# Down projection blocks of seven products: product 3 inside the chain, and six more low parts per group made by ScalarE and an accumulating transfer

## The chip, the cores and the metric

The kernel runs on one core of a Trainium2 chip, in one launch. The metric is the device time of an execution in microseconds. A core has a matrix engine (PE), a vector engine (DVE), a scalar engine (ACT), GpSimd (POOL) and a synchronising engine (SP). They run at the same time, each one through its own list of instructions in order, and wait for each other by semaphores. SP issues the loads of weights, POOL the transfers that add to what is in their destination. PE writes to PSUM, in banks that other engines read.

## The reference

Two layers, each an attention-like mixing part and a gated feed-forward part, on 512 tokens of width 1024, all in float32. The change is in the feed-forward part, which both layers have:

```python
f = rmsnorm(h, ln_ffn_pre[layer])
f = (jax.nn.silu(f @ w_ffn_gate[layer]) * (f @ w_ffn_up[layer])) @ w_ffn_down[layer]
h = h + rmsnorm(f, ln_ffn_post[layer])
```

The hidden width D_FF is 2816, 22 blocks of 128.

## The kernel before

**Parts.** PE is fed with pairs of tiles: a float32 tile is split into a high part that PE's input format holds (whi, fhi) and a low part, the rest (wlo, flo). A product of two such pairs is three matmuls: high by high, high by low, low by high (`mm3`, lines 191 to 193). The usual split (`split`, line 239) is a cast on ACT and a subtraction on DVE. A second form (`split_aside`, lines 1151 to 1153) leaves DVE out: ACT casts, ACT writes the negated high part into the low tile, and POOL issues a transfer that adds the source to it. Before, only the last two of the four splits of the first pair in a group are made that way. Pairs of weights lie in eight buffers that are used in turn, so they can be made eight ahead of PE.

**Blocks of seven.** Gate, up and down products are 2 by 2 blocks, multiplied with seven block products instead of eight (after Winograd). Two hidden blocks with all eight blocks of width are one `Seven` for gate and one for up: their raw weights come by SP into tiles raw, DVE forms sums and differences of the four quadrants (lines 1041 to 1046), and PE makes product 1, 7, 2, 6, 4, 3, 5 in this order; product 7, into tile e, needs the parts of the difference s3.

**Groups.** Hidden blocks 2 to 21 are taken in five groups of four. A group is two pairs of Sevens; in the first four groups a down block of seven (`down_sevens`) follows, which adds the group's share of the result into eight tiles y, of 128 tokens by 512 columns (ys[token block][half]; ys[0][0], ys[0][1], ys[1][0], ... are y_2471 to y_2478 in the first layer). Two layers make eight such down blocks. The block has two units: a for the first pair of hidden blocks, whose raw weights come in tiles raw, and b for the second, with four tiles wd. `Inner.combine` makes the activations' sums and parts, `DownSeven` the weights'. A product of a unit is six matmuls 512 wide, onto two PSUM banks: chain (yc), shared (ys), lows (yl) and, before, ups (yu).

**Getting sums out.** `put` copies a bank to a tile yo on ACT and lets POOL issue one accumulating transfer of 256 KB for each tile y that the sum belongs to (line 1229). `final` adds a bank to its y tile on DVE (line 1232); where a put into that y tile is under way, DVE waits for it to land.

**The order** on each engine is fixed when the kernel is built, by a scheduler that goes by data and buffers and by the order in which the code is written; PE and DVE may get rows of different products interleaved. Transfers of POOL are issued in the order of its list.

Of the kernel before, what the change touches and what calls it, by code (L numbers as in the profile page):

```python
# [40 lines left out]
def hybrid(ctx: ExitStack, tc: tile.TileContext, i: dict, out: bass.AP):  # L41
# [20 lines left out]
    def plain(s, shape=(P, T), dt=F32):  # L62
        return yp.tile(list(shape), dt, tag="y", name=name(s))
# [174 lines left out]
    def split(src, hi, lo, eng=None):  # L238
        last_parts[:] = A.copy(hi, src), (eng or V).tensor_sub(lo, src, hi)  # L239
# [873 lines left out]
    def feed_forward(layer, phase, xp, meanwhile=None):  # L1113
# [34 lines left out]
        def split_aside(src, hi, lo, aside):  # L1148
            if not aside:
                return split(src, hi, lo)  # L1150
            A.copy(hi, src)
            A.activation(lo, hi, AF.Copy, scale=-1.0)
            G.dma_start(lo, src, accum_op=ALU.add)

        class Inner:

            def __init__(self, k, aside):
                self.k, self.aside, self.u = k, aside, {}

            def __call__(self, row, u):  # L1160
                self.u[row] = u
# [3 lines left out]
            def combine(self, u0, u1):  # L1165

                left, right = (slice(*c) for c in HALVES)
                first = tp.tile([P, 2, 256], F32R, tag="acc", name=name("b11"), bufs=2)
                split(u0[:, left], first[:, 0, :], first[:, 1, :])
                second, both, other = [(act("fhi"), act("flo")) for _ in range(3)]  # L1170
                split(u1, *second)
                V.tensor_sub(u0[:, left], u0[:, right], u0[:, left])
                V.tensor_sub(u0[:, right], u1[:, right], u0[:, right])
                V.tensor_sub(u1[:, right], u0[:, left], u1[:, right])
                V.tensor_add(u1[:, left], u1[:, right], u1[:, left])
                split_aside(u0, *both, self.aside)
                split_aside(u1, *other, self.aside)
                half = lambda pair, c: tuple(t[:, c] for t in pair)
                self.x = {1: (first[:, 0, :], first[:, 1, :]), 2: half(second, left), 3: half(second, right),
                          4: half(other, left), 5: half(both, left), 6: half(other, right), 7: half(both, right)}  # L1180

        class DownSeven:

            def __init__(self, pair, spare):
                self.x = pair.x
                if spare:
                    a11, a12, a21, a22 = (plain("wd").rearrange("p (m c) -> p m c", m=4) for _ in range(4))
                    for n, a in enumerate((a11, a12, a21, a22)):
                        last_load[0] = nc.sync.dma_start(
                            a, i["w_down"][layer, 4 * (n // 2) : 4 * (n // 2) + 4, :, pair.k + n % 2, :].rearrange("m p c -> p m c"))  # L1190
                else:
                    raws = []
                    for dh in range(2):
                        raw = wp.tile([P, 1024], F32, tag="raw", name=name("raw"), bufs=4)
                        last_load[0] = nc.sync.dma_start(
                            raw.rearrange("p (m c) -> p m c", m=4),
                            i["w_down"][layer, 4 * dh : 4 * dh + 4, :, pair.k : pair.k + 2, :].rearrange("m p k c -> p m (k c)"))
                        raws.append(raw.rearrange("p (m k c) -> p m k c", m=4, k=2))
                    a11, a12, a21, a22 = (r[:, :, x, :] for r in raws for x in range(2))
                self.w = {4: a22}  # L1200
# [4 lines left out]
                self.w[2] = self.parts(a12)  # L1205
                V.tensor_sub(a11, a11, a21)
                V.tensor_add(a12, a11, a12)
                self.w.update({3: a12, 5: a21, 6: a11, 7: s3})

            def parts(self, src):  # L1210
                pair = pair_of_parts()
                split(src, *(t.rearrange("p (m c) -> p m c", m=4) for t in pair))
                return pair

            def product(self, outs, n, start, stop):
                w = self.w[n]
                if n > 2:
                    w = self.parts(w)
                for x, o in enumerate(outs):
                    c = slice(x * P, (x + 1) * P)  # L1220
                    mm3(o, tuple(t[:, c] for t in self.x[n]), w, start, stop, True)

        def down_sevens(pairs):

            def put(x, *where):
                some = prob("yo")
                A.copy(some, x)  # L1227
                for tb, dh in where:
                    G.dma_start(ys[tb][dh], some, accum_op=ALU.add)  # L1229

            def final(x, tb, dh):
                V.tensor_add(ys[tb][dh], x, ys[tb][dh])

            a, b = DownSeven(pairs[0], False), None
            chain = [ps("tr", s="yc") for _ in range(2)]
            a.product(chain, 1, True, False)
            lows = [ps("mm", s="yl") for _ in range(2)]
# [24 lines left out]
            b.product(chain, 5, False, True)  # L1262
            for x in range(2):
                put(chain[x], (x + 2, 0), (x + 2, 1))
            b.product(shared, 4, False, True)
            for x in range(2):
                final(shared[x], x, 1)

        fs = [(act("fhi"), act("flo")) for _ in range(2)]

# [19 lines left out]
                A.copy(ys[tb][dh], o)  # L1290

        for gi, (k0, k1) in enumerate(groups):
            fs, pairs = [], []
            for m in range(k0, k1, 2):
                if meanwhile and m == k1 - 2 and gi == len(groups) - 1:
                    next(meanwhile)
                if gi < len(groups) - 1:
                    pairs.append(Inner(m, m < k1 - 2))
# [19 lines left out]
            down_sevens(pairs)  # L1318


    def layer_b(phase, fp):
# [297 lines left out]
```

## Time and profile before

| what | value |
|---|---|
| median of 3 runs | 1107.26 us (1107.19 to 1495.4) |
| profiled execution, its own time | 1105.52 us |
| its span, first to last instruction | 1103.8 us |
| mean granted clock of PE in it | 0.995 |
| PE busy | 1082.3 us (98%) |
| DVE busy | 972.7 us (88%) |
| ACT busy | 752.5 us (68%) |
| POOL busy | 107.5 us (10%) |
| accumulating puts y<-yo | 80, of 256 KB, 7.4 us from issue to landing (median) |
| low parts flo by transfer | 16, of 256 KB, 3.3 us (median) |

A row of a group of instructions reads: line, engine, operation, output<-inputs, how often; durations in ns (smallest, median, largest) or busy us and mean ns; then the idle time before and what ended it. A row of the timeline reads: start and duration in us, engine, line, operation, tiles, count, and in brackets the idle time before it and what ended it. A row of waits reads: engine and line, what it waited for, us in total, number of waits, the longest.

### The profile page before, as it was taken

How to read it: one execution, taken by the hardware profiler on the slowest of the kernel's cores; microseconds unless marked ns; L12 is line 12 of the kernel's file. 1: busy time of each engine (PE TensorE's matmuls, PEld its weight loads, DVE VectorE, ACT ScalarE, POOL GpSimd, SP SyncE). 2: the span in 40 equal slices, each digit the busy share in tenths (PEclk: the TensorE clock that was granted, in tenths of full speed). 3: DMA queues.
4: the chain of work that ended last, by engine and by line, in shares of the span. 5: the costliest groups of instructions: out<-in, count | busy, mean ns of one | idle time of the engine just before them, and what ended most of it. 6: DMA issues, size and time to landing. Idle time of an engine off the chain costs nothing.

```text
span 1103.8 us, 19831 instructions
## 1 busy us (share of the span) xinstructions
PE 1082.3 (98%) x7266; PEld 986.1 (89%) x7267; DVE 972.7 (88%) x1942; ACT 752.5 (68%) x1588; POOL 107.5 (10%) x136
## 2 busy tenths in 40 slices
PE   9999999999999999899999999999999999999998
PEld 8998889998979898898988998889997989899996
DVE  7879759899989999897967789968999999999986
ACT  7776578666656667577846788868666756666664
POOL 0000000003030212101000000000003020210200
PEclk9999999999999999999999999999999999999999
DMA  7521331338474573836122555541347566383832
GB/s 269 161 79 58 115 115 39 115 96 210 134 159 144 123 206 92 204 133 204 44 91 77 139 133 134 141 127 39 98 113 161 145 148 178 86 220 96 188 118 77
DMA packets 86297, 143.85 MB, mean 130 GB/s; under 512 B 7028, under 2 KB 50056, under 8 KB 86200
## 3 DMA queue, kind: packets, MB, share of 16 engines
q1 hardware_dynamic: 71480, 116.57, 34.1%
q0 software_dynamic: 14016, 25.70, 13.1%
q8 instruction: 57, 0.93, 0.3%
q10 hardware_dynamic: 704, 0.32, 0.1%
q14 instruction: 40, 0.33, 0.1%
HBM read 105.23 MB, written 2.10 MB: 97 GB/s over the span
## 4 chain that ended last, share of the span: by engine, by line
PE 77%; DVE 10%; DMA 6%; ACT 3%; issue 2%; POOL 1%; SPq 0%; DVEq 0%; ACTq 0%
DMA y<-yo 5%; PE y L191 5%; PE y L192 5%; PE y L193 4%; PE a L191 4%; PE a L192 4%; PE a L193 4%; PE ps L191 4%; PE ps L193 4%; PE ps L192 4%; PE e L193 3%; DVE wlo L239 3%; PE e L192 3%; PE e L191 3%; PE x L192 3%; PE x L193 3%
## 5 line engine op out<-in xcount | busy, mean ns | idle before, releaser
L239 ACT CAST whi<-raw 128x512 fp32r<-128x512 f32 x444 | 260.4, 619 | 116.1 <-DVE raw L1045 46.2
L239 DVE TENSOR_TENSOR wlo<-raw,whi 128x512 fp32r<-128x512 f32 x444 | 291.9, 687 | 20.4 <-ACT whi L239 19.8
L192 PE MATMUL x<-xslo,whi 128*128 128x256 f32 x320 | 90.6, 283 | 0.0
L191 PE MATMUL x<-xshi,whi 128*128 128x256 f32 x320 | 90.5, 283 | 0.0
L193 PE MATMUL x<-xshi,wlo 128*128 128x256 f32 x320 | 90.3, 282 | 0.0
L191 PE MATMUL a<-xshi,whi 128*128 128x256 f32 x320 | 89.9, 281 | 0.0
L192 PE MATMUL a<-xslo,whi 128*128 128x256 f32 x320 | 89.8, 281 | 0.0
L193 PE MATMUL a<-xshi,wlo 128*128 128x256 f32 x320 | 89.7, 280 | 0.0
L1229 POOL DMA_DIRECT2D y<-yo x80 | 69.4, 1147 | 195.3 <-ACT yo L1227 173.2
L191 PE MATMUL ps<-xshi,whi 128*128 128x256 f32 (+1 forms) x224 | 68.4, 305 | 0.0
L192 PE MATMUL ps<-xslo,whi 128*128 128x256 f32 (+1 forms) x224 | 66.7, 298 | 0.0
L193 PE MATMUL ps<-xshi,wlo 128*128 128x256 f32 (+1 forms) x224 | 66.3, 297 | 0.0
L193 PEld LDWEIGHTS x<-xshi,wlo 128*128 128x128 f32 x320 | 61.1, 191 | 0.0
L192 PEld LDWEIGHTS x<-xslo,whi 128*128 128x128 f32 x320 | 60.9, 190 | 0.0
L191 PEld LDWEIGHTS x<-xshi,whi 128*128 128x128 f32 x320 | 60.9, 190 | 0.0
L192 PEld LDWEIGHTS a<-xslo,whi 128*128 128x128 f32 x320 | 60.2, 188 | 0.4
L191 PEld LDWEIGHTS a<-xshi,whi 128*128 128x128 f32 x320 | 60.2, 188 | 0.4
L193 PEld LDWEIGHTS a<-xshi,wlo 128*128 128x128 f32 x320 | 60.3, 188 | 0.0
L193 PE MATMUL e<-t3hi,wlo 128*128 128x256 f32 x160 | 46.5, 290 | 12.6 <-DVE wlo L239 12.6
L239 ACT CAST whi<-s 128x512 fp32r<-128x512 f32 x56 | 34.8, 622 | 24.6 <-DVE s L1041 15.4
L191 PE MATMUL y<-whi,mixedhi 128*128 128x512 f32 x128 | 51.3, 400 | 0.0
L192 PE MATMUL y<-wlo,mixedhi 128*128 128x512 f32 x128 | 50.5, 395 | 0.0
(358 smaller groups left out, 3645.0 us busy)
## 6 DMA issues: line engine op xcount, KB each, us to landing
raw<-in_w_gate SPq DMA_DIRECT2D x44, 512.0 KB, 3.9
raw<-in_w_up SPq DMA_DIRECT2D x44, 512.0 KB, 4.2
y<-yo POOLq DMA_DIRECT2D x80, 256.0 KB, 7.4
raw<-in_w_down SPq DMA_DIRECT2D x28, 512.0 KB, 4.6
raw<-in_w_out SPq DMA_DIRECT2D x16, 512.0 KB, 3.8
wd<-in_w_down SPq DMA_DIRECT2D x32, 256.0 KB, 10.5
flo<-s POOLq DMA_DIRECT2D x16, 256.0 KB, 3.3
raw<-in_w_b_q SPq DMA_DIRECT2D x8, 512.0 KB, 4.6
```

What stands on the lines that cost most here:

```text
L191: PE.matmul(o, w[0], x[0], start=start, stop=False, skip_group_check=more)
L192: PE.matmul(o, w[0], x[1], start=False, stop=False, skip_group_check=more)
L193: return PE.matmul(o, w[1], x[0], start=False, stop=stop, skip_group_check=more)
L239: last_parts[:] = A.copy(hi, src), (eng or V).tensor_sub(lo, src, hi)
L1229: G.dma_start(ys[tb][dh], some, accum_op=ALU.add)
```

## The change

Product 3 gets no banks of its own any more. It comes last and is added to the chain, after the chain's sum (products 1, 6 and 5) has been put out to ys[x+2][1]; the chain with product 3 then goes by a final addition into ys[x+2][0]. So the put of the sum 1, 6, 5 has one destination instead of two, and a group has eight puts instead of ten. Products are ordered anew; before b's first product stand three products of a (1, 7, 2) instead of four (1, 2, 7, 3). The sum that product 3 needs, a11 + a12, is formed in `product` once product 2's parts are made. The loads of b's four wd tiles are written ahead of the second pair of Sevens instead of inside the down block.

In each group six low parts change from DVE to ACT and POOL: the other two of the first pair's four splits in `Inner`, and the weights' parts of products 3 and 4 of both units. The latter read raw or wd; in raw, rows of 128 numbers lie apart from each other (128x4x128), in wd they lie together. Before DVE may write on u0 and u1 in `Inner`, the transfers that read them must have landed.

```diff
                 first = tp.tile([P, 2, 256], F32R, tag="acc", name=name("b11"), bufs=2)
-                split(u0[:, left], first[:, 0, :], first[:, 1, :])
+                split_aside(u0[:, left], first[:, 0, :], first[:, 1, :], self.aside)
                 second, both, other = [(act("fhi"), act("flo")) for _ in range(3)]
-                split(u1, *second)
+                split_aside(u1, *second, self.aside)
...
-            def parts(self, src):
+            def parts(self, src, aside=False):
                 pair = pair_of_parts()
-                split(src, *(t.rearrange("p (m c) -> p m c", m=4) for t in pair))
+                split_aside(src, *(t.rearrange("p (m c) -> p m c", m=4) for t in pair), aside)
                 return pair
 
             def product(self, outs, n, start, stop):
                 w = self.w[n]
-                if n > 2:
+                if n == 2:
                     w = self.parts(w)
+                    V.tensor_add(self.a[1], self.a[0], self.a[1])
+                    self.w[3] = self.a[1]
+                elif n != 1:
+                    w = self.parts(w, n in (3, 4))
...
+            a, b = us
+            a.sums(pairs[0])
+            chain, shared, lows = ([ps(t, s=n) for _ in range(2)] for t, n in (("tr", "yc"), ("lg", "ys"), ("mm", "yl")))
             a.product(chain, 1, True, False)
+            a.product(shared, 7, True, False)
             a.product(lows, 2, True, False)
-            shared = [ps(t, s="ys") for t in ("mm", "lg")]
-            a.product(shared, 7, True, False)
-            ups = [ps(t, s="yu") for t in ("lg", "lg")]
-            a.product(ups, 3, True, False)
-            b = DownSeven(pairs[1], True)
+            b.sums(pairs[1])
             b.product(chain, 1, False, True)
             for x in range(2):
                 put(chain[x], (x, 0))
             b.product(shared, 7, False, True)
             for x in range(2):
                 put(shared[x], (x, 1), (x + 2, 1))
-            for u in (a, b):
-                u.product(chain, 6, False, u is b)
+            both(chain, 6)
+            with tc.high_priority():
+                for x in range(2):
+                    A.copy(shared[x], chain[x])
+            b.product(lows, 2, False, True)
+            both(chain, 5)
             for x in range(2):
-                A.copy(shared[x], chain[x])
-            b.product(ups, 3, False, True)
+                put(chain[x], (x + 2, 1))
             for x in range(2):
-                final(ups[x], x + 2, 0)
-            a.product(chain, 5, False, False)
-            a.product(shared, 4, False, False)
-            b.product(lows, 2, False, True)
+                V.tensor_add(ys[x][0], lows[x], ys[x][0])
+            both(shared, 4)
             for x in range(2):
-                final(lows[x], x, 0)
-            b.product(chain, 5, False, True)
+                V.tensor_add(ys[x][1], shared[x], ys[x][1])
+            both(chain, 3)
             for x in range(2):
-                put(chain[x], (x + 2, 0), (x + 2, 1))
-            b.product(shared, 4, False, True)
-            for x in range(2):
-                final(shared[x], x, 1)
+                V.tensor_add(ys[x + 2][0], chain[x], ys[x + 2][0])
```

`both` runs a product of a and then of b.

How the lists move is shown in the third group of the first layer. POOL's list there, before, holds the ten puts of the down block:

```order
L1229 DMA y_2471<-yo_4779 128x512
L1229 DMA y_2473<-yo_4782 128x512
L1229 DMA y_2472<-yo_4795 128x512
L1229 DMA y_2476<-yo_4795 128x512
L1229 DMA y_2474<-yo_4799 128x512
L1229 DMA y_2478<-yo_4799 128x512
L1229 DMA y_2475<-yo_4875 128x512
L1229 DMA y_2476<-yo_4875 128x512
L1229 DMA y_2477<-yo_4879 128x512
L1229 DMA y_2478<-yo_4879 128x512
```

And now, with the low parts of product 4 (raw_4711 for a, wd_4413 for b) and of product 3 (raw_4709, wd_4411):

```order
L1234 DMA y_2471<-yo_4768 128x512
L1234 DMA y_2473<-yo_4771 128x512
L1153 DMA wlo_4854<-raw_4711 128x4x128
L1153 DMA wlo_4865<-wd_4413 128x512
L1234 DMA y_2472<-yo_4784 128x512
L1234 DMA y_2476<-yo_4784 128x512
L1234 DMA y_2474<-yo_4788 128x512
L1234 DMA y_2478<-yo_4788 128x512
L1153 DMA wlo_4878<-raw_4709 128x4x128
L1153 DMA wlo_4889<-wd_4411 128x512
L1234 DMA y_2476<-yo_4845 128x512
L1234 DMA y_2478<-yo_4848 128x512
```

The low part of a's product 3 is the ninth transfer of the block. Six of the eight groups have this order. In the first group of each layer the four low parts stand at places 7, 8, 9 and 12, behind the six puts.

PE's list of the changed kernel, at the turn from product 4 of b (ys) to product 3 of a (yc), where the tiles of those transfers are read:

```order
L191 MATMUL ys_4724<-whi_4864,fhi_4697 128x512
L192 MATMUL ys_4724<-wlo_4865,fhi_4697 128x512
L193 MATMUL ys_4724<-whi_4864,flo_4698 128x512
L191 MATMUL yc_4721<-whi_4877,fhi_4391 128x512
L192 MATMUL yc_4721<-wlo_4878,fhi_4391 128x512
L193 MATMUL yc_4721<-whi_4877,flo_4392 128x512
L191 MATMUL yc_4722<-whi_4877,fhi_4391 128x512
L192 MATMUL yc_4722<-wlo_4878,fhi_4391 128x512
L193 MATMUL yc_4722<-whi_4877,flo_4392 128x512
L191 MATMUL yc_4721<-whi_4888,fhi_4693 128x512
L192 MATMUL yc_4721<-wlo_4889,fhi_4693 128x512
```

The first read of wlo_4878 stands 51 rows behind the last matmul of b's product 1 on yc_4721, whose sum is the first put; the first reads of the two low parts of product 4 stand 39 and 45 rows behind it. In the first group of a layer the first read of the last of the four stands 64 rows behind. Before, DVE wrote the tiles that stand at these places.

DVE's list, before, behind the down block: the final additions from ys stand ahead of the low part of s3 (wlo_4931), which the next Seven's tile e waits for:

```order
L1041 TENSOR_TENSOR s_19_4904<-raw_4895,raw_4897 128x512
L239 TENSOR_TENSOR wlo_4907<-raw_4895,whi_4906 128x512
L1043 TENSOR_TENSOR raw_4897<-raw_4897 128x512
L239 TENSOR_TENSOR wlo_4912<-raw_4895,whi_4911 128x512
L1232 TENSOR_TENSOR y_2472<-ys_4728,y_2472 128x512
L1232 TENSOR_TENSOR y_2474<-ys_4729,y_2474 128x512
L1045 TENSOR_TENSOR raw_4895<-raw_4897,raw_4895 128x512
L239 TENSOR_TENSOR wlo_4931<-s_19_4904,whi_4930 128x512
```

And now (the low part of s3 is wlo_4937):

```order
L239 TENSOR_TENSOR wlo_4913<-raw_4901,whi_4912 128x512
L1045 TENSOR_TENSOR raw_4901<-raw_4903,raw_4901 128x512
L239 TENSOR_TENSOR wlo_4918<-raw_4901,whi_4917 128x512
L1046 TENSOR_TENSOR raw_4901<-raw_4901 128x512
L239 TENSOR_TENSOR wlo_4937<-s_19_4910,whi_4936 128x512
L239 TENSOR_TENSOR wlo_4966<-raw_4901,whi_4965 128x512
L1265 TENSOR_TENSOR y_2472<-ys_4723,y_2472 128x512
L1265 TENSOR_TENSOR y_2474<-ys_4724,y_2474 128x512
```

The two additions have moved behind the low part of s3 and the one after it.

More of the change, by code (lines that the diff above doesn't have):

```diff
@@ L1155, in feed_forward, with __init__ @@
         class Inner:
-            def __init__(self, k, aside):
-                self.k, self.aside, self.u = k, aside, {}
+            def __init__(self, aside):
+                self.aside, self.u = aside, {}
             def __call__(self, row, u):
@@ L1182, in feed_forward, with __init__ @@
         class DownSeven:
-            def __init__(self, pair, spare):
-                self.x = pair.x
+            def __init__(self, k, spare):
                 if spare:
-                    a11, a12, a21, a22 = (plain("wd").rearrange("p (m c) -> p m c", m=4) for _ in range(4))
-                    for n, a in enumerate((a11, a12, a21, a22)):
+                    self.a = [plain("wd").rearrange("p (m c) -> p m c", m=4) for _ in range(4)]
+                    for n, a in enumerate(self.a):
                         last_load[0] = nc.sync.dma_start(
-                            a, i["w_down"][layer, 4 * (n // 2) : 4 * (n // 2) + 4, :, pair.k + n % 2, :].rearrange("m p c -> p m c"))
+                            a, i["w_down"][layer, 4 * (n // 2) : 4 * (n // 2) + 4, :, k + n % 2, :].rearrange("m p c -> p m c"))
                 else:
@@ L1196, in __init__, with sums @@
                             raw.rearrange("p (m c) -> p m c", m=4),
-                            i["w_down"][layer, 4 * dh : 4 * dh + 4, :, pair.k : pair.k + 2, :].rearrange("m p k c -> p m (k c)"))
+                            i["w_down"][layer, 4 * dh : 4 * dh + 4, :, k : k + 2, :].rearrange("m p k c -> p m (k c)"))
                         raws.append(raw.rearrange("p (m k c) -> p m k c", m=4, k=2))
-                    a11, a12, a21, a22 = (r[:, :, x, :] for r in raws for x in range(2))
-                self.w = {4: a22}
+                    self.a = [r[:, :, x, :] for r in raws for x in range(2)]
+            def sums(self, pair):
+                self.x = pair.x
+                a11, a12, a21, a22 = self.a
+                self.w = {2: a12, 4: a22}
                 s3 = temp("s3").rearrange("p (m c) -> p m c", m=4)
@@ L1204, in __init__ @@
                 V.tensor_add(a21, a21, a22)
-                self.w[2] = self.parts(a12)
                 V.tensor_sub(a11, a11, a21)
-                V.tensor_add(a12, a11, a12)
-                self.w.update({3: a12, 5: a21, 6: a11, 7: s3})
-            def parts(self, src):
+                self.w.update({5: a21, 6: a11, 7: s3})
+            def parts(self, src, aside=False):
                 pair = pair_of_parts()
-                split(src, *(t.rearrange("p (m c) -> p m c", m=4) for t in pair))
+                split_aside(src, *(t.rearrange("p (m c) -> p m c", m=4) for t in pair), aside)
                 return pair
@@ L1221, in product, with down_sevens @@
                     mm3(o, tuple(t[:, c] for t in self.x[n]), w, start, stop, True)
-        def down_sevens(pairs):
+        def down_sevens(us, pairs):
             def put(x, *where):
@@ L1229, in put, with both @@
                     G.dma_start(ys[tb][dh], some, accum_op=ALU.add)
[L1231 to L1235, printed above, removed]
+            def both(outs, n):
+                a.product(outs, n, False, False)
+                b.product(outs, n, False, True)
+            a, b = us
+            a.sums(pairs[0])
+            chain, shared, lows = ([ps(t, s=n) for _ in range(2)] for t, n in (("tr", "yc"), ("lg", "ys"), ("mm", "yl")))
             a.product(chain, 1, True, False)
-            lows = [ps("mm", s="yl") for _ in range(2)]
+            a.product(shared, 7, True, False)
             a.product(lows, 2, True, False)
-            shared = [ps(t, s="ys") for t in ("mm", "lg")]
-            a.product(shared, 7, True, False)
-            ups = [ps(t, s="yu") for t in ("lg", "lg")]
-            a.product(ups, 3, True, False)
-            b = DownSeven(pairs[1], True)
+            b.sums(pairs[1])
             b.product(chain, 1, False, True)
@@ L1292, in feed_forward @@
         for gi, (k0, k1) in enumerate(groups):
-            fs, pairs = [], []
+            fs, pairs, downs = [], [], []
             for m in range(k0, k1, 2):
@@ L1297, in feed_forward @@
                 if gi < len(groups) - 1:
-                    pairs.append(Inner(m, m < k1 - 2))
+                    pairs.append(Inner(m < k1 - 2))
+                    if m > k0:
+                        downs.append(DownSeven(m, True))
                 else:
@@ L1317, in feed_forward @@
                                layer == 1)
-            down_sevens(pairs)
+            down_sevens([DownSeven(k0, False)] + downs, pairs)
     def layer_b(phase, fp):
```

## The prediction

> **What bounds the kernel now.** First the busy times of the page, to see which engine has no slack.
>
> ```profile
> span 1103.8 us, 19831 instructions
> PE 1082.3 (98%) x7266; PEld 986.1 (89%) x7267; DVE 972.7 (88%) x1942; ACT 752.5 (68%) x1588; POOL 107.5 (10%) x136
> ```
>
> PE is busy for 98% of the span, and the change neither adds nor removes a matmul. What can be won is PE's idle time, 1103.8 - 1082.3 = 21.5 us, and what a slowed clock costs. What can be lost has no such ceiling. So the second view is what PE waited for.
>
> ```profile
> PE e L193 <- DVE wlo L239: 12.6, 7, 3.0
> PE ys L191 <- ACT fhi L239: 1.4, 2, 0.7
> PE yc L192 <- DVE wlo L239: 1.1, 2, 0.5
> ```
>
> The same view, asked for the stretch around each down block, puts six of the seven waits at e there:
>
> ```profile
> PE e L193 <- DVE wlo L239: 0.6, 1, 0.6
> ...
> PE e L193 <- DVE wlo L239: 2.7, 1, 2.7
> ...
> PE e L193 <- DVE wlo L239: 0.9, 1, 0.9
> ...
> PE e L193 <- DVE wlo L239: 3.0, 1, 3.0
> ...
> PE e L193 <- DVE wlo L239: 1.6, 1, 1.6
> ...
> PE e L193 <- DVE wlo L239: 2.5, 1, 2.5
> ```
>
> They sum to 11.3 us. Right behind the block the next group's first Seven runs product 7 (tile e) before its low part exists. The timeline behind the second down block shows why.
>
> ```profile
> 325.68 0.69 DVE L1232 TENSOR_TENSOR y<-ys,y 128x512 f32<-128x512 f32 x1 [3.12 <-DMA y<-yo]
> 326.29 0.68 DVE L1045 TENSOR_TENSOR raw<-raw,raw 128x512 f32<-128x512 f32 x1
> 326.88 0.69 DVE L239 TENSOR_TENSOR wlo<-s,whi 128x512 fp32r<-128x512 f32 x1
> ...
> 327.62 0.58 PE L193 MATMUL e<-t3hi,wlo 128*128 128x256 f32 x1 [2.74 <-DVE wlo L239]
> ```
>
> DVE stood 3.12 us in the final addition to y[1][1], because an accumulating put into the same tile had not landed. The low part of s3 came next but one behind it, and PE stood 2.74 us. So this wait is not a lack of DVE throughput: DVE takes its work in order, and a late transfer held it. After the three long ones the clock fell.
>
> ```profile
> 318.00:334.00 16.00, 13.26 (x81) 12.23 (x80) 11.62 (x20) 6.55 (x13) 3.46 (x4) 0.89 1.11 256
> 445.00:461.00 16.00, 13.04 (x87) 12.36 (x86) 11.14 (x19) 6.99 (x14) 3.46 (x4) 0.89 1.03 258
> 905.00:921.00 16.00, 13.51 (x87) 12.66 (x86) 11.62 (x21) 6.48 (x14) 3.42 (x4) 0.89 1.08 264
> ```
>
> PEclk, third from the end, is 0.89 in each: (1 - 0.89) x 16 = 1.76 us of clock lost per drop, 5.3 us in all.
>
> Now the resource that the change leans on, the queue of accumulating transfers behind POOL: its issues in the second block, their landings, the same for two later groups of puts (the put of 315.57 and that of 324.82 are the latest of their rows), and a low part made this way in a quiet place.
>
> ```profile
> 310.36 1.75 POOL L1229 DMA_DIRECT2D y<-yo  x2 [16.17 <-ACT yo L1227]
> 313.93 3.51 POOL L1229 DMA_DIRECT2D y<-yo  x4 [1.83 <-ACT yo L1227]
> 321.36 0.85 POOL L1229 DMA_DIRECT2D y<-yo  x1 [3.91 <-ACT yo L1227]
> 324.27 1.74 POOL L1229 DMA_DIRECT2D y<-yo  x2 [2.07 <-DMA y<-yo]
> ...
> L1229 POOL DMA_DIRECT2D y<-yo x3: 1197/1530/1877, 314.5 to 315.6; - x3
> DMA to landing us min/median/max: 9.5/10.6/11.6
> ...
> L1229 POOL DMA_DIRECT2D y<-yo x2: 865/1031/1197, 324.3 to 324.8; - x2
> DMA to landing us min/median/max: 6.9/7.3/7.7
> ...
> L1153 POOL DMA_DIRECT2D flo<-s x1: 853/853/853, 354.8 to 354.8; - x1
> DMA to landing us min/median/max: 3.3/3.3/3.3
> ```
>
> Alone, 256 KB land 3.3 us after issue. In the block the sixth put lands 11.6 us after its own issue, 315.57 + 11.6 - 310.36 = 16.8 us after the first one's, and the ninth 324.82 + 7.7 - 310.36 = 22.2 us after it. The landings come in the order of issue, about 2 us apart. So the transfers stand in one line, and what is issued last waits for all before it.
>
> ```profile
> q0 software_dynamic: 14016, 25.70, 13.1%
> ...
> q0 software_dynamic: 1131, 2.08, 56.2%
> q1 hardware_dynamic: 2318, 2.06, 34.5%
> ```
>
> The columns are packets, MB and share of 16 engines. The first row is the page's: 25.70 MB are 98 pieces of 256 KB, and 0.131 x 1103.8 / 98 = 1.48 us is what one takes of all 16 engines. The other two are for 309 to 330 us: the accumulating queue filled 56.2%, weight loads 34.5%. That is why 1.48 us becomes 2.
>
> **The change part by part.** Edits with one answer first. Two puts fewer per group (16 in all) and product 3 carried on in the chain instead of in two banks of its own: no PE work, the same six copies to yo and six final additions. Six low parts per group leave DVE:
>
> ```profile
> L239 DVE TENSOR_TENSOR wlo<-raw,whi 128x512 fp32r<-128x512 f32 x444 | 291.9, 687 | 20.4 <-ACT whi L239 19.8
> ...
> L239 DVE TENSOR_TENSOR flo<-f,fhi x8: 417/424/427, 186.7 to 781.2; 128x256 fp32r<-128x256 f32 x8
> L1152 ACT ACTIVATE flo<-fhi x16: 626/632/635, 230.8 to 1002.2; 128x512 fp32r<-128x512 f32 x16
> ```
>
> Five at 687 ns and one half as wide save DVE 5 x 0.69 + 0.42 = 3.9 us per group; ACT gets six negations in their place, at most 6 x 0.63 = 3.8 us, and is 68% busy. Both lie beside PE's work and are costed at nothing; their cover is the eight pairs of buffers by which the parts run ahead. If ACT lost that lead, the cost would be those 3.8 us per group.
>
> *The two low parts in Inner.* They now land before DVE may overwrite their sources. That pair is combined one pair of Sevens ahead of the down block, some 20 us, against 3.3 us for a transfer alone: nothing, at most 3.3 us per group.
>
> *The wait at e.* In the new order the low part of s3 stands ahead of the final additions that can stall. I take all of it back: 11.3 us and the three clock drops, 16.6 us. Late next are the inputs of b: three products of a stand ahead of them, not four, so 6 x 0.23 = 1.4 us less cover (matmul spacing below). The two small waits above show that there is little slack there; DVE's shorter list works the other way. I take 0, between 1.4 us lost and 0.3 us won per group.
>
> *The wait that is added.* The low parts of products 3 and 4 now come through the line of transfers. In six of eight groups it holds two puts, the low parts of product 4, four puts, and only then that of a's product 3, as ninth. PE's cover between the first put and that need:
>
> ```profile
> 241.63 0.39 PE L191 MATMUL yc<-whi,b 128*128 128x512 f32 x1
> ...
> 242.32 0.40 PE L191 MATMUL yc<-whi,b 128*128 128x512 f32 x1
> ...
> 249.83 1.07 ACT L1227 COPY yo<-yc 128x512 f32<-128x512 f32 x2
> ...
> 250.70 1.73 POOL L1229 DMA_DIRECT2D y<-yo  x2 [16.00 <-ACT yo L1227]
> ```
>
> Three starts lie between 241.63 and 242.32, 0.23 us apiece. From the last matmul of b's product 1 on the first chain tile to the first one that reads the ninth transfer's tile are 51 rows: 51 x 0.2325 = 11.9 us. The put goes out when that matmul ends (0.40) and the copy is made (250.70 - 249.83 = 0.87): 1.3 us later. Cover: 10.6 us.
>
> Supply, from below: with no loads beside it the ninth lands 3.3 + 8 x 1.48 = 15.1 us after the first put. From above: the row of the ninth put, 22.2 us, where POOL twice waited (3.91 and 2.07 us) while the line was still draining. I take 19.5 us, nearer to the row, because the loads of the next group run in the same stretch, though one of them now waits for a landing: (19.5 - 3.3) / 8 = 2.03 us a transfer. PE waits 19.5 - 10.6 = 8.9 us (4.5 to 11.6). Product 4's low parts, third and fourth, land 3.3 + 2 x 2.03 = 7.4 us and 9.4 us after the first put; PE comes to them after 39 and 45 rows, 7.8 and 9.2 us after it: nothing. The tenth follows the ninth by 2.0 us, while PE spends 6 x 0.23 = 1.4 us on a product, more at a slower clock: nothing more. A wait this long drops the clock as the three above did: 1.8 us. Together 10.7 us.
>
> In the first group of each layer both product-4 parts stand behind all six puts, and b's product 3 is twelfth: it lands at 3.3 + 11 x 2.03 = 25.6 us. The cover there is 64 rows, 14.9 - 1.3 = 13.6 us. Wait 12.0, clock 1.8, together 13.8 us.
>
> What stands behind the waiting matmul is the whole next group, since PE takes its work in order; DVE and ACT use the pause to get ahead, but PE cannot win the time back.
>
> Two of the nine transfers read raw in rows of 128 numbers, four short rows for each long one. At worst a short row costs as much as a long one: 3 x 1.48 = 4.4 us more apiece, 8.9 us per group; at best nothing. I take nothing: the reading side alone changes. The Trainium skill, "DMA: Bandwidth & Descriptors", section "Why small descriptors are slow (HBM only)", says that transfers within SBUF do not suffer from small pieces. By that the worst case would not come; no row here shows it either way.
>
> The sum: 6 x 10.7 + 2 x 13.8 - 16.6 = +75.2 us on the profiled execution's 1105.5 us, so 1180.7; the median of the runs, 1107.3, lies 1.7 us above that execution. I say **1182 us**.
>
> **The rivals.** *The line drains faster than PE arrives.* If the ninth lands within the cover of 10.6 us, which is a transfer each (10.6 - 3.3) / 8 = 0.9 us, no wait comes and only the gain is left: 1107.3 - 16.6 = 1091 us, not slower. For it: alone, a transfer lands in 3.3 us, and PE's list of waits names no transfer today. Against it: the least that a transfer took of the engines is 1.48 us, and the landings of 11.6 us. The Trainium skill, same page, section "Anatomy of one DMA — SWDGE (gpsimd) path", fits a transfer as 2.0 us plus its bytes at 436 GB/s, which makes 0.6 us for 256 KB. By that, an estimate, the ninth would land after 2.6 + 8 x 0.6 = 7.4 us and this rival would hold; the rows of 1.48 us and 11.6 us disagree.
>
> *Loads stay away.* At 1.48 us each the wait is 4.5 us in six groups and 3.3 + 11 x 1.48 - 13.6 = 6.0 us in two: 6 x 6.3 + 2 x 7.8 - 16.6 = +36.8, 1144 us. For it: loads of the next group wait for the low parts to release their buffers. Against it: two pairs of loads do not.
>
> *Short rows cost in full.* +8.9 us in eight groups, 71 us on top: 1253 us. For it: nothing but the number of pieces; against it: bytes, not pieces, set the 1.48 us of a put.
>
> *The change gives DVE time that nobody needs.* Then the waits at e would stay, 16.6 us more than the forecast, 1199 us. The new order speaks against it.
>
> **How the numbers follow.** Forecast 0.60, with 1199 in it; loads away 0.20; short rows 0.08; fast line 0.12. The range takes in the first two with their bounds and leaves out the last two, 0.20. Its low end is loads away without the clock loss and with 0.3 us won at b's inputs, 1144 - 8 x 2.1 = 1127 us. Its high end has a ninth landing after 22.2 us (11.6 us of wait; for the twelfth 15.7) and 1.4 us lost at b's inputs: 6 x 14.8 + 2 x 18.9 - 16.6 = +110, and one group in two with 2 us for Inner's parts, 1225 us. A measurement of this kernel tells some 2% from no change, 1085 to 1129 us. Slower than that: 0.60 + 0.08 + most of 0.20 = 0.85. The fast line at 1091 us is within it: 0.12. Faster by over 2% would need 22 us, more than all of PE's idle time without the clock: 0.03.
>
> **What would show it.** Right: in each down block PE waits about 9 us for a transfer into wlo just ahead of product 3; the waits of e for DVE are gone; PEclk falls below 1 in eight places, not three; the landings of wlo from raw come 8 us and more after issue. The e waits still there would refute the gain; landings of wlo near 3.3 us in the block would refute the loss, and the fast line would have it. Waits that sit at product 4 already would mean that short rows cost more than I allow.

## The result, and the profile after

The changed kernel takes **1198.2 us** (median; 1197.1 to 1199.9), the kernel before 1107.2 us: a ratio of 1.0825 with a 95% interval of 1.0808 to 1.0842, 91 us slower. The forecast was 1182 us, with a range of 1127 to 1225. (One execution of the kernel before, 1495.4 us, lies far from all others and is left out of the ratio.)

The page of the kernel after, its span and busy times (us, share of the span, instructions):

```profile
span 1198.2 us, 20155 instructions
PE 1110.3 (93%) x7266; PEld 997.7 (83%) x7267; DVE 952.6 (80%) x1894; ACT 777.0 (65%) x1636; POOL 142.4 (12%) x168
```

DVE did get less to do, 20.1 us, and ACT 24.5 us more. PE does the same matmuls and was idle for 1198.2 - 1110.3 = 87.9 us, where it was 21.5 us: 66.4 of the 94.4 us by which the span grew. The rest, 28.0 us, stands as busy time. What PE waited for, in the kernel after (engine, line, what it waited for: us in total, times, the longest):

```profile
PE yc L192 <- DMA wlo<-raw: 44.8, 6, 8.4
PE ys L192 <- DMA wlo<-raw: 9.5, 2, 4.8
PE yc L192 <- DMA wlo<-wd: 6.8, 2, 4.0
PE yc L193 <- DVE flo L239: 5.8, 6, 2.2
PE e L191 <- ACT s L1074: 4.9, 8, 1.2
PE yc L191 <- ACT ys L1256: 3.4, 8, 0.5
```

The waits of e for DVE, the largest of before, are gone. In their place PE waits 44.8 + 9.5 + 6.8 = 61.1 us for low parts of weights that come by a transfer. The six of the first row are one for each steady group, at product 3 of a. The second block shows how one comes about. First POOL's issues in the timeline:

```profile
325.45 1.72 POOL L1234 DMA_DIRECT2D y<-yo  x2 [12.47 <-ACT yo L1232]
327.50 1.28 POOL L1153 DMA_DIRECT2D wlo<-raw  x1 [0.34 <-DVE flo L239]
328.26 1.42 POOL L1153 DMA_DIRECT2D wlo<-wd  x1
329.54 3.64 POOL L1234 DMA_DIRECT2D y<-yo  x4
331.68 2.79 POOL L1153 DMA_DIRECT2D wlo<-raw  x1
334.33 1.05 POOL L1153 DMA_DIRECT2D wlo<-wd  x1
```

The view of line 1153 for the last two of these, and PE's first matmul in the timeline that reads the ninth transfer's tile:

```profile
DMA to landing us min/median/max: 12.5/13.2/14.0
```

```profile
345.71 0.79 PE L192 MATMUL yc<-wlo,fhi 128*128 128x512 f32 x1 [7.64 <-DMA wlo<-raw]
```

Two puts, two low parts (product 4), four puts, and as ninth and tenth the two low parts of product 3. Of the two landings the longer is the earlier transfer's: it is issued at 331.68 and lands 14.0 us later, at 345.7, when PE starts. POOL had no idle time ahead of its issue; it stood behind eight others. From the first issue to the ninth landing are 345.7 - 325.45 = 20.2 us. The queues in the stretch 325 to 346 us (packets, MB, share of 16 engines) and the median landings there:

```profile
q0 software_dynamic: 2248, 2.71, 86.9%
q1 hardware_dynamic: 1728, 1.31, 21.5%
...
wlo<-raw POOLq DMA_DIRECT2D x2, 256.0 KB, 9.8
wlo<-wd POOLq DMA_DIRECT2D x2, 256.0 KB, 9.4
```

The accumulating queue's packets take 86.9% of the engines' time in these 21 us, and with the loads' 21.5% the rows come to 108%: packets overlap, and no share is left free. 0.869 x 21 us over 2.71 MB, 10.3 pieces of 256 KB, is 1.77 us apiece. The short rows of raw make no visible difference beside wd (9.8 and 9.4 us; each is the middle of two, the third and ninth in the line and the fourth and tenth). The Trainium skill, "DMA: Bandwidth & Descriptors", section "Why small descriptors are slow (HBM only)", says that this penalty does not apply within SBUF; these two rows agree.

PE's clock in the same place, two of the eight blocks in windows of 16 us (PEclk is third from the end):

```profile
408.00:424.00 16.00, 8.60 (x29) 6.74 (x28) 6.13 (x10) 3.45 (x7) 1.69 (x2) 0.68 1.10 235
484.00:500.00 16.00, 8.57 (x32) 6.87 (x31) 5.52 (x9) 2.70 (x6) 1.69 (x2) 0.68 1.04 230
```

0.68 where the drops of before showed 0.89. A part of the slow stretch lies in the wait itself, where it costs nothing. The rest does cost: in the first of these two blocks the wait ends at 417.8, and until 424 PE works at 0.50.

```profile
417.80:424.00 6.20, 6.16 (x18) 5.09 (x19) 1.75 (x3) 1.24 (x2) 0.00 (x0) 0.50 1.03 282
```

How much of that can be won back is one of the questions below.

### The profile page after: what moved, and what is told of

Its sections match the earlier page's. It is cut to its first block, busy times and chain, and to the rows that moved or that the text cites. A ratio compares the mean times of both kernels' runs of the same rounds, so it can differ in the third digit from the quotient of the medians.

```text
span 1198.2 us, 20155 instructions
## 1 busy us (share of the span) xinstructions
PE 1110.3 (93%) x7266; PEld 997.7 (83%) x7267; DVE 952.6 (80%) x1894; ACT 777.0 (65%) x1636; POOL 142.4 (12%) x168
## 5 line engine op out<-in xcount | busy, mean ns | idle before, releaser
L239 ACT CAST whi<-raw 128x512 fp32r<-128x512 f32 x428 | 257.8, 620 | 210.4 <-PE yc L193 79.9
L239 DVE TENSOR_TENSOR wlo<-raw,whi 128x512 fp32r<-128x512 f32 x428 | 285.3, 684 | 40.2 <-ACT whi L239 39.0
L192 PE MATMUL yc<-wlo,fhi 128*128 128x512 f32 x96 | 45.1, 470 | 51.6 <-DMA wlo<-raw 44.8
L191 PE MATMUL a<-xshi,whi 128*128 128x256 f32 x320 | 91.4, 286 | 0.0
L193 PE MATMUL a<-xshi,wlo 128*128 128x256 f32 x320 | 91.0, 285 | 0.0
L191 PE MATMUL x<-xshi,whi 128*128 128x256 f32 x320 | 90.0, 281 | 0.0
L193 PE MATMUL x<-xshi,wlo 128*128 128x256 f32 x320 | 89.8, 281 | 0.0
L1234 POOL DMA_DIRECT2D y<-yo x64 | 57.8, 1262 | 149.8 <-ACT yo L1232 88.3
L192 PEld LDWEIGHTS yc<-wlo,fhi 128*128 128x128 f32 x96 | 21.6, 225 | 58.6 <-DMA wlo<-raw 47.4
L191 PE MATMUL ps<-xshi,whi 128*128 128x256 f32 (+1 forms) x224 | 68.3, 305 | 0.0
L193 PE MATMUL ps<-xshi,wlo 128*128 128x256 f32 (+1 forms) x224 | 66.3, 298 | 0.0
L191 PEld LDWEIGHTS a<-xshi,whi 128*128 128x128 f32 x320 | 62.0, 194 | 0.9
L193 PEld LDWEIGHTS a<-xshi,wlo 128*128 128x128 f32 x320 | 61.9, 194 | 0.2
L1153 POOL DMA_DIRECT2D flo<-s x24 | 20.5, 856 | 341.3 <-ACT flo L1152 202.9
L193 PEld LDWEIGHTS x<-xshi,wlo 128*128 128x128 f32 x320 | 60.4, 189 | 0.0
L191 PEld LDWEIGHTS x<-xshi,whi 128*128 128x128 f32 x320 | 60.3, 189 | 0.0
L191 PE MATMUL y<-whi,mixedhi 128*128 128x512 f32 x128 | 51.4, 401 | 0.0
```

What stands on the lines that cost most here:

```text
L191: PE.matmul(o, w[0], x[0], start=start, stop=False, skip_group_check=more)
L192: PE.matmul(o, w[0], x[1], start=False, stop=False, skip_group_check=more)
L193: return PE.matmul(o, w[1], x[0], start=False, stop=stop, skip_group_check=more)
```

## The experiments

The theory: the low parts of the weights stand in one line with the puts, and PE waits for the line. Its rivals: the new order costs by itself; a transfer is late by a delay of its own, wherever it stands; the slow clock carries a good part. Ratios are to the kernel before, run on the same chip. The expectations call DVE VectorE, ACT ScalarE and PE the matmul unit.

### Which part of the change costs the time

First, the kernel after without the weights' transfers:

```diff
-                    w = self.parts(w, n in (3, 4))
+                    w = self.parts(w)
```

> The changed kernel with the four weights' low parts of products 3 and 4 back on DVE; the new order of products, the eight puts and Inner's transfers stay. If the loss is PE's wait for the ninth and tenth (twelfth) transfer of POOL's line and the half clock behind it, every wait of PE for a transfer into wlo goes, PEclk stays at 1.0, and the time is 1090 to 1107 us. If the new order (b's inputs needed 1.4 us sooner) or Inner's transfers carry the loss, it stays above 1125 us.

Second, the kernel before with the change's two further low parts in `Inner` alone (`split` becomes `split_aside` for the first pair and for u1):

> The kernel before with Inner's two more low parts by transfer and nothing else. If the weights' transfers carry the loss: 1103 to 1113 us, with DVE waiting up to 3.3 us per group for them to land (14.6 us in eight waits were seen in the changed kernel) and PE hardly at all. If Inner carries a part of the loss: over 1120 us.

Third, the kernel after without either, so that the new order and the two puts fewer per group are left. (The expectation speaks of eight sums that are no longer carried out; in fact 16 transfers fewer are issued, two in each of eight groups, and no sum is missing.)

> The kernel after with every low part made by VectorE's subtraction as before: neither the weights of products 3 and 4 nor the Inner blocks use an accumulating transfer, so what is left of the change is the new order of the products and the eight sums that are no longer carried out. My theory (nearly all of the loss is the wait for the weights' transfers): with those gone the time is near the kernel before, and the fewer sums give VectorE time back, so 1100 to 1115 us; the matmul unit's waits for VectorE's subtraction, 11.3 us before, are back in some part. The rival (the new order costs by itself, which the 1117 us of the run without the weights' transfers leaves possible): 1115 to 1130 us, with the copies by ScalarE of the sums (line 1074) as the largest waits. If the Inner transfers and the order each take their share of those 10 us, as the run of the Inner transfers alone (1111 us) says, this run lies at 1111 to 1115 us.

Fourth, the order and the weights' transfers without those of `Inner`:

> The kernel after with the low parts of the Inner blocks' first two pairs made by VectorE's subtraction: the new order and the aside low parts of products 3 and 4 stay. The new order alone measured 1.001 of the kernel before, the order with the Inner transfers 1.008, all three 1.082. My theory (the costs add): the Inner transfers' 7 to 10 us go, 1186 to 1194 us. The rival (the Inner transfers' waits lie inside the longer wait at product 3, since the matmul unit is late for all of it): no gain, 1195 to 1200 us.

| kernel | median, us | ratio, 95% interval |
|---|---|---|
| before with the two in Inner | 1110.9 | 1.0033 [1.0021, 1.0045] |
| new order alone | 1106.8 | 1.0013 [1.0002, 1.0025] |
| order and Inner | 1117.0 | 1.0077 [1.0055, 1.0098] |
| order and weights | 1189.9 | 1.0753 [1.0723, 1.0782] |
| all three (after) | 1198.2 | 1.0825 [1.0808, 1.0842] |

In 1107 us the weights' transfers are worth (1.0825 - 1.0077) x 1107 = 83 us with Inner's, and (1.0753 - 1.0013) x 1107 = 82 without. The order costs 1.4 us, and the rival that it costs more by itself is out. The two in `Inner` cost 7 us on top of the new order, 8 on top of order and weights, and 3.7 us in the kernel before. The first of these kernels was expected at 1107 us at most and came at 1117, since I had given Inner's transfers no price; the fourth came inside what was expected of it.

That 82 and 83 agree is no proof that the costs simply add, for the fourth kernel waits at other places. PE's waits for transfers in it:

```profile
PE ys L192 <- DMA wlo<-wd: 28.5, 4, 7.7
PE ys L192 <- DMA wlo<-raw: 20.3, 5, 5.2
PE yc L192 <- DMA wlo<-wd: 11.8, 6, 3.3
PE yc L192 <- DMA wlo<-raw: 8.2, 2, 4.3
```

48.8 of these 68.8 us are at product 4, where the steady groups of the kernel after have none. POOL's list differs: in four groups the low part of b's product 4 stands behind the four shared puts, as eighth, and in the other four both low parts of product 4 stand behind all four. So here too PE waits for whatever stands far back in the line.

What Inner's two do shows in PE's waits, here of the kernel before with the two alone:

```profile
PE e L191 <- ACT s L1074: 13.2, 15, 1.6
PE ys L191 <- ACT fhi L239: 3.4, 4, 1.1
```

The waits for DVE at e are gone there too. The bank e is now late for another reason: ACT has not copied out what stood in it. That this comes of the two negated parts more that ACT makes in each group is how I read it; no run takes them away alone. PE loses as much as it did for DVE, though the expectation had PE wait hardly at all. In the kernel after, DVE also stands for these transfers before it may write on u0 and u1:

```profile
DVE s L1172 <- DMA b<-s: 14.6, 8, 3.3
```

### Is it the line, or the transfer?

In the next two kernels only one product's weights are made aside, which changes the place in the line. `n == 3` in the one, `n == 4` in the other:

```diff
-                    w = self.parts(w, n in (3, 4))
+                    w = self.parts(w, n == 3)
```

> The kernel after with the low parts of product 4's two weights made by VectorE's subtraction; only product 3's two, which stand seventh and eighth of the POOL queue's transfers, are made aside. My theory (the wait is the place in the line: some 1.7 us of the engines' time for each transfer ahead): both products' own copies land two places earlier than in the kernel after for the one that is last in line, and product 4 waits for no transfer; the wait of product 3 of a falls from 7.4 to 8.4 us to 3 to 6 us, six times, and the time to 1145 to 1175 us. The rival (each transfer has its fixed delay, whatever stands ahead): the same waits as in the kernel after, 1190 to 1200 us.

> The kernel after with the low parts of product 3's two weights made by VectorE's subtraction; only product 4's two are made aside, which are needed earlier on the matmul unit or later in the line as the order of the products has it. My theory (the line's place against the time of need): whichever of the two is issued behind fewer puts waits less; product 4's transfers go out ahead of product 3's in the kernel after, so a wait of 0 to 3 us each and 1105 to 1150 us. The rival (an accumulating transfer is late by its own duration, wherever it stands): waits of 5 us and more at product 4 and 1160 to 1185 us.

Measured: product 3 alone 1163.1 us, ratio 1.0523 [1.0499, 1.0546]; product 4 alone 1147.2 us, ratio 1.0373 [1.0348, 1.0397]. Both lie in the range of the line's theory. PE's waits for transfers, the first row of the kernel with product 3, the second of that with product 4:

```profile
PE yc L192 <- DMA wlo<-raw: 32.8, 8, 6.3
...
PE ys L192 <- DMA wlo<-raw: 13.1, 2, 7.0
```

With product 3 alone the transfer stands seventh instead of ninth. The wait in the second block shows what that does:

```profile
336.73 0.50 PE L192 MATMUL yc<-wlo,fhi 128*128 128x512 f32 x1 [3.80 <-DMA wlo<-raw]
```

3.80 us where it was 7.64: two places are 3.8 us. With product 4 alone the transfers stand third and fourth in six groups, and there PE waits for none; in the first group of each layer they stand behind all six puts, and there it waits 13.1 us in two. The same transfer is in time or six to seven microseconds late by its place. Not all of this kernel's 41 us are such waits: 8 are Inner's, 13 these two, and the remaining 20 I only find in pieces (PE's waits at a for ACT's copies at line 1071, 6.3 us, and PE's busy time, 7.7 us more than with no weights aside).

The strongest form of the test takes the puts out of the line:

```diff
-                put(shared[x], (x, 1), (x + 2, 1))
+                put(shared[x])
...
-                put(chain[x], (x + 2, 1))
+                put(chain[x])
```

> The kernel after with the six accumulating puts of a group that stand ahead of the low parts of product 3 in the POOL queue's line left out (the four of the shared copies and the two of product 5; ScalarE's copies for them stay): six sums of each group are missing from the output. All low parts are still made aside. My theory (what the matmul unit waits for is the length of the line ahead, some 1.7 us for each transfer): six transfers fewer are 10 us, more than the 7.4 to 8.4 us waited at product 3 of a, so that wait is gone in the steady groups and what is left are the half-clock windows and the small waits: 1112 to 1140 us. The rival (an accumulating transfer is late by its own delay, the line ahead counts little): the waits at product 3 stay above 5 us and the time above 1165 us.

Measured 1132.0 us, ratio 1.0220 [1.0187, 1.0252]. PE's waits for transfers in this kernel:

```profile
PE yc L192 <- DMA wlo<-wd: 5.9, 5, 2.6
...
PE yc L192 <- DMA wlo<-raw: 2.3, 4, 0.9
...
PE ys L192 <- DMA wlo<-raw: 0.5, 2, 0.2
```

With the row of `ys` 61.1 us have become 8.7, though every low part is still made by a transfer. Six puts fewer per group gave back 66 us. The rival of a fixed delay is out.

### Can the line be put in another order?

The kernel after with the six puts issued behind the low parts of product 3, cut (the two late puts are held back in the same way, and the two additions from `shared` are written behind all of them):

```diff
-                put(shared[x], (x, 1), (x + 2, 1))
+                some = prob("yo")
+                A.copy(some, shared[x])
+                held.append(some)
...
+            both(chain, 3)
+            with tc.issue_after(last_low[0].ins):
+                for x in range(2):
+                    for tb in (x, x + 2):
+                        G.dma_start(ys[tb][1], held[x], accum_op=ALU.add)
```

> The changed kernel with the same transfers, but the four shared puts and the two late puts issued behind the low part of b's product 3: the four low parts stand third to sixth in the line. If the place in the line makes the wait, the fifth lands about 3.3 + 4 x 1.8 = 10.5 us after the first put, against a cover of 10.6 us: PE waits at most 1 to 2 us at product 3, time 1095 to 1125 us. If a transfer of its own is slow (short rows, ACT's negation late), the wait of some 7.4 us stays, over 1160 us.

Measured 1160.1 us, ratio 1.0469 [1.0451, 1.0487]: better than the kernel after by 38 us, and far from the 1095 to 1125 that I expected. PE's waits, and below them DVE's and one of ACT's:

```profile
PE e L191 <- ACT s L1074: 19.3, 15, 3.7
PE yc L192 <- DMA wlo<-wd: 6.3, 6, 1.5
...
PE yc L192 <- DMA wlo<-raw: 2.9, 4, 1.2
...
DVE y L1280 <- DMA y<-yo: 48.1, 15, 5.6
...
DVE y L1270 <- DMA y<-yo: 14.6, 13, 2.6
...
ACT whi L239 <- DVE s L1041: 38.7, 9, 6.2
```

The waits for low parts fell to 9.7 us (0.5 of them at product 4), as their new place says. But now the puts are last in the line, and DVE's final additions stand 62.7 us for them. Behind these stand DVE's sums of the next group (s, line 1041), behind these ACT's parts, and in ACT's row the copies out of e that PE waits for, 19.3 us. That is how I read the rows, and the kernel without the six puts bears it out: its low parts stand at the same places and wait much the same, 8.7 us, but DVE's 48.1 us are gone, ACT's 38.7 us have become 1.7, e's 19.3 us have become 5.0, and the time is 28 us lower. What part of the 28 us comes from the additions' later place in the program, and not from the puts, no run tells. The line has not become shorter, and whoever is last in it stops somebody who works in order.

### What the slow clock costs

The kernel after with 26 matmuls that add zero, put where PE waits, so that the clock falls less:

```diff
+            for _ in range(26):
+                PE.matmul(chain[0], neg[:, :P], neg, start=False, stop=False, skip_group_check=True)
             both(chain, 3)
```

> The changed kernel with 26 matmuls of zeros, 512 wide, added to the chain ahead of product 3: 26 x 0.23 = 6.0 us of work that changes no sum, within a wait of 7.4 us. If the idle wait drops the clock and that costs PE some 28 us of slower matmuls, PEclk stays near 1.0 and the time falls by 15 to 28 us, to 1170 to 1183 us. If the clock costs little beside the line, 1195 us or more.

Measured 1195.9 us, ratio 1.0796 [1.0778, 1.0813]: 2 to 3 us better. The mean granted clock rose from 0.966 to 0.988, the wait at product 3 was largely filled, and another grew:

```profile
PE e L191 <- ACT s L1074: 8.9, 15, 1.2
PE yc L192 <- DMA wlo<-raw: 8.5, 5, 2.2
```

e waits 8.9 us for ACT's copies where it was 4.9: what the faster clock wins behind the landing is in part waited for again at the next place. The fill has a price of its own, too. In the first group of each layer it takes 2 x 6.0 us where PE waited 6.8 us at product 3, so some 5 us are lost there. Without the fill PE's busy time is 1145.5 - 8 x 26 x 0.2325 = 1097.1 us, 13 us less than in the kernel after; this is an estimate, and it leaves other slow stretches in place. So this fill won 2 to 3 us, not the 15 to 28 us that I expected, but it does not show that the slow clock is worth no more: some 13 us of slow work went, and 4 + 5 us of waiting and overlong fill came for them.

### The gain that the change was near to, by itself

What the change did win, the waits at e, came from a put that held DVE. That put stood fifth in the line of the block, since the puts of copy 0 to both its tiles went ahead of those of copy 1. In the kernel before, with only their order altered:

```diff
+            some = [prob("yo") for _ in range(2)]
             for x in range(2):
-                put(shared[x], (x, 1), (x + 2, 1))
+                A.copy(some[x], shared[x])
+            for n in range(4):
+                G.dma_start(ys[n][1], some[n % 2], accum_op=ALU.add)
```

> The kernel before with only the issue order of the shared copies' four puts changed: the four accumulating puts go out as copy 0, 1, 2, 3 of the sums where they went out as 0, 2, 1, 3, so the put that VectorE's second final addition waits for lands one place earlier. My theory (VectorE's low part of the next group's product is late because VectorE is held at its final addition by that put, which shows as 11.3 us of waits of the matmul unit and three half-clock windows): one place in the line is some 1.7 us, most of those waits go, 1092 to 1104 us. The rival (VectorE is late by its own work, the wait for the put is beside it): 1105 to 1110 us, no change.

And the same edit in the kernel with the new order alone:

> The kernel with the new order alone and no additional aside low part, and with the four shared puts issued as copy 0, 1, 2, 3, the edit that took the kernel before from 1106 to 1092.5 us. My theory (the same final addition of VectorE holds the low part that the matmul unit waits for; its waits were 10.3 us in the new order alone): 1088 to 1100 us. If the eight sums fewer on VectorE are worth anything once the put is no longer late, it is below 1092; the rival (in the new order the final additions stand elsewhere in VectorE's row and the put's place is beside it): 1103 to 1110 us.

The kernel before with the puts swapped: **1092.5 us**, ratio 0.9879 [0.9858, 0.9900]. The new order with the puts swapped: **1091.7 us**, ratio 0.9867 [0.9845, 0.9889]. Both beat both kernels. The views of the former, PE's wait and DVE's:

```profile
PE e L193 <- DVE wlo L239: 5.3, 4, 1.5
...
DVE y L1232 <- DMA y<-yo: 4.5, 3, 1.9
```

PE's was 12.6 us, and DVE's row, quoted here from the kernel before, was

```profile
DVE y L1232 <- DMA y<-yo: 13.1, 7, 3.4
```

Of the new order with the puts swapped, the page's busy times, and then PE's wait at e:

```profile
PE 1078.7 (99%) x7266; PEld 981.0 (90%) x7267; DVE 971.4 (89%) x1942; ACT 753.8 (69%) x1588; POOL 93.7 (9%) x120
```

```profile
PE e L193 <- DVE wlo L239: 0.8, 1, 0.8
```

PE is busy for 99% and its clock is full in all of it but the end (mean 1.000). That the two intervals overlap says that the two puts fewer in each group add nothing that these runs can tell once the late put is early. (Nor does DVE have eight sums fewer in the new order, as the expectation says: its count is 1942 in this kernel and in the kernel before.)

## Why the prediction was right, and where it was not

**What bounds the kernel: right.** PE had 21.5 us of idle time and a little clock to give; the best kernel found by these runs wins 14.7 us. Taking 20 us of work off DVE did end the waits of e for DVE, but won no time; in the kernel before with Inner's two alone, PE waits as long for ACT. That DVE was late by a held addition, and not by its amount of work, shows where the puts are swapped: DVE is busy for 972.6 us as before, and 13.4 us are won.

**The added wait: right in place and cause, its size a little high.** It sits just ahead of a's product 3 in the six steady groups, and the ninth landing comes 20.2 us after the first put in the second block; 19.5 were forecast, from rows of the kernel before alone. The wait is 7.5 us (44.8 / 6) and not 8.9. The term that was off is the cover: 20.2 - 7.6 = 12.6 us in the second block, not 10.6, because PE came later. In that block it waited 0.8 us at `yc L193` for DVE's flo, an input of b, and 0.5 us at `yc L191` for ACT's copy into ys; the remaining 0.7 us stay open, and are not a slow clock, which was granted in full from 325 to 338 us. I had named those inputs as late next and priced them at 0, between 1.4 us lost and 0.3 won. The reason given for 2 us a transfer, the loads beside it, is not borne out: in the block of the kernel before one took 0.562 x 21 us / 7.9 = 1.49 us beside loads of 34.5%, and here 1.77 us beside 21.5%.

**The first group of each layer.** 12.0 us each were forecast, at the twelfth transfer. Measured are (9.5 + 6.8) / 2 = 8.2 us, split over product 4 (4.7 and 4.8) and product 3 of b (2.8 and 4.0). I said that waits at product 4 would mean costlier short rows. In the steady groups there are none; in these two groups, product 4 waits because it stands behind six puts, which I used for product 3 and did not work out for product 4.

**The clock.** 8 x 1.8 = 14.4 us were forecast as lost, after drops to 0.89; in the steady groups they were drops to 0.68. By busy time the term was too small: PE's is 21.3 us above that of the kernel without the weights' transfers (1110.3 and 1089.0). Where a part of it was taken away by the fill, only 2 to 3 us came back as time.

**The two in Inner at nothing: wrong.** They cost 7 to 8 us here. The time shows in PE's waits at e for ACT's copies, 9.1 us in the kernel with order and Inner; DVE stands 14.6 us for the transfers, but that this is behind it is not shown. The bound, 3.3 us per group, holds (26 us).

**The wait at e, -16.6 us: right in size, wrong in reason.** The waits went, but not because of the new order: with it alone they are back at 10.3 us. In the kernel with the new order and nothing else, DVE's row has the final addition ahead of the low part of s3, as before:

```profile
326.62 0.69 DVE L1265 TENSOR_TENSOR y<-ys,y 128x512 f32<-128x512 f32 x1 [2.15 <-PE yc L193]
...
330.23 0.68 DVE L239 TENSOR_TENSOR wlo<-s,whi 128x512 fp32r<-128x512 f32 x1
```

The row names PE as what ended the addition's wait, but with the puts swapped in this same order the wait at e falls from 10.3 to 0.8 us: it was the put. It took the moved low parts to end the waits otherwise. The size nearly holds: the swapped puts, which change the order of four issues, win 13.4 to 14.7 us.

**The sum.** By kernels: weights +83, Inner +7, order +1, together the +91 measured. The forecast had 6 x 10.7 + 2 x 13.8 = +92 for the weights, 0 and -16.6. It was 16 us short: 9 too much for the weights, 7 too little for Inner, 18 too little for the order, whose gain it booked and the order alone does not bring. These steps are net: the end of e's waits for DVE lies inside Inner's +7, beside the new waits for ACT. Within the weights, 77.4 us of waiting were forecast and 61.1 measured, 14.4 us of slow clock and 21.3 of busy time; that the two nearly make up for each other is luck. The rival that the time saved on DVE serves nobody named 1199 us, the time that was measured, but not for its reason: the waits at e did not stay.

**The other rivals.** *The line drains fast* is out: 1.77 us a transfer in the block, not 0.9. The Trainium skill, "DMA: Bandwidth & Descriptors", section "Anatomy of one DMA — SWDGE (gpsimd) path", has a transfer take its bytes at 436 GB/s beyond a fixed 2.0 us, by which 256 KB would be 0.6 us, an estimate; here one took about three times that in the line. *Loads stay away* is half right: the loads took 21.5% of the engines in the block's stretch and not 34.5%, but the line still needed 20.2 us to the ninth landing, where that rival has 15.1. *Short rows in full* is out.

## What to carry to other kernels

Work that is moved off a busy engine into a queue gets the queue's length as its delay: count what stands ahead of it at the moment of need, and count that the thing behind it gets later by as much. An engine at 88% that makes the bound engine wait may be held by one late input; then look at the order of the transfers into it first, for an edit of a few lines there won 13 to 15 us, where a change that moved 20 us of its work lost 91. And a transfer that is added on one side reads or writes buffers that somebody else waits for: price that wait too, even when there are 20 us of distance.

## What the runs showed of the hardware

An accumulating transfer of 256 KB between tiles held the 16 engines 1.77 us each in a full line, and the ninth in the line of the second block landed 14.0 us after its issue, against 3.3 us alone. A wait of 7.4 us of PE left the granted clock at 0.68 over 16 us, 0.50 in the 6.2 us of work behind it; a fill that raised the mean clock from 0.966 to 0.988 was worth only 2 to 3 us of 1198. The order of four issues, on a queue that moves the same bytes, was worth 1.2% of the whole kernel.
